# Sparse attention with large and small query tiles in turn, lower weight parts in pieces, last squares summed on TensorE

## The chip, the cores and the metric

The kernel runs on one core of a Trainium2 chip. The metric is device time in microseconds (us), the median of several executions of the whole program. Five queues work side by side: TensorE (PE, with its weight loads as PEld), VectorE (DVE), ScalarE (ACT), GpSimd (POOL) and SyncE (SP, which issues the DMAs).

## What is computed

One decoder layer on x of 1024 tokens by 1024 channels, in fp32: a norm, one input projection for three mixers (a chunked state-space scan, stick-breaking attention, sparse attention), gates that merge them, an output projection, a norm and a residual; then a gated MLP with a short convolution, and again a norm and a residual. Cut to the parts that the change touches:

```
def nsa_attention(...):            # sparse attention, 8 query heads, 2 key groups, head size 64
    ...
    imp = jnp.where(valid, jnp.where(forced, BIG, imp), NEG)
    _, idx = lax.top_k(imp, n_sel)             # 8 selected blocks of 64 keys
    p_sel = masked_softmax(ss, ...)            # over the selected blocks
    o_win = ... masked_softmax(sw, wmask) ...  # over a window of 512 keys
    out = gb[..., 0] * o_cmp + gb[..., 1] * o_sel + gb[..., 2] * o_win

def reference(...):
    ...
    x = x + rms_norm(mixed @ w_out[l], post_mix_norm[l])
    h = rms_norm(x, pre_ffn_norm[l])
    u = causal_dwconv(h @ ffn_w_up[l], ffn_conv_w[l], ffn_conv_b[l])
    gate, val = jnp.split(u, 2, axis=-1)
    f = (jax.nn.gelu(gate, approximate=True) * val) @ ffn_w_down[l]
    x = x + rms_norm(f, post_ffn_norm[l])
```

## The kernel before

Activations lie with channels on the partitions and tokens along the free axis, in halves of 512 tokens. A product of two fp32 matrices is made of three matmuls: each operand is split into an upper part (`hi`, rounded to TensorE's fp32 format) and a lower part (`lo`, the rest), and hi·hi, lo·hi and hi·lo are summed in PSUM. In the trace these are the matmuls called `dense`, 128x512 each.

**Weights.** `load_w` (line 278) brings a block of weights by a DMA of SP, makes `whi` on ACT (line 286) and `wlo` on POOL by one subtraction over the whole block (line 287): 78 blocks of 128x1024 and 16 of 128x512. A block of 1024 columns holds eight weight tiles of 128x128; its products take 24 matmuls, in which every third uses `wlo`. Some other weights have code of their own (`weights7`, from line 513); the change leaves that alone.

**Sparse attention** (`nsa_stage`, some 460 to 803 us). There are 16 query tiles of 128 queries: two key groups g, eight tiles i = 0 to 7 in each. Tile i attends to i + 1 blocks of 128 keys in the selected branch and to at most five in the window branch, so the tiles have 2, 4, 6, 8, 10, 11, 12 and 13 key blocks. Three pieces of program run interleaved, in an order written out by the loop over n behind line 1047: `attend` works on tile n (scores by TensorE, exponentials on ACT, `wT_lo` on POOL, products with the values on TensorE, merging on DVE), `maxima` on tile n + 1 and `compressed` on tile n + 2. `compressed` has the attention over compressed keys and, for i of 4 and more, the top-k chain on DVE (lines 888 to 900). `maxima` computes, for each head and branch, the products of queries and keys once more and takes their largest value on DVE (`mx`, line 955): 8 pieces for i below 4 and 16 for larger i; then `MM` (lines 962 and 963), three steps of delay (`MM_LAG`), four small transposes on TensorE and a copy into the rows of `Q` (line 969). Without these rows no score of the tile can start.

A tile gets max(9, its blocks) slots. In each slot `maxima` takes two steps and `compressed` one. What remains of either when the slots are over runs at once. Slots with no block are filled with matmuls of the merge gates' projection (`fill`, six matmuls, or three where a slot has a block and both other pieces are done); these wait for nothing in this stage. Instructions stand on each engine in the order in which the loop records them, so the order of the tiles sets what stands in front of what.

**Output projection, MLP and last norm** (`tail_stage`). `rstd` sums squares over the partitions with a matmul by ones, then takes Ln and Exp on ACT (lines 1483 and 1484) and three operations on DVE. The last part of the last product runs over three column groups, `LAST`, of 512, 256 and 256 columns. For each, eight output tiles j: the x add on DVE (line 1820), a square on ACT (1825), the sum of squares on DVE (1826), a scale on ACT (1827). `start_norm` of a group stands inside the next group's loop (the last one behind it): `norm_rows` turns the column sums into one number per token by small matmuls, takes the root on 128x2 or 128x4 values (lines 253 to 258), spreads it (1792) and transposes it back (`psn<-ident,u`); then eight multiplies on DVE (1803) and eight adds of the residual on POOL or DVE (1804), each followed by its DMA out.

Of the kernel before, what the change touches and what calls it, by code (L numbers as in the profile page):

```python
# [10 lines left out]
F32 = mybir.dt.float32  # L11
R32 = mybir.dt.float32r
BF = mybir.dt.bfloat16
AF = mybir.ActivationFunctionType
OP = mybir.AluOpType
# [4 lines left out]
T = 1024  # L20
DM = 1024
# [170 lines left out]
U0_BUFS = 6  # L192
U1_BUFS = 2
# [17 lines left out]
def trunk(ctx: ExitStack, tc: tile.TileContext, A: dict, outT: bass.AP, dbg=None):  # L211
    nc = tc.nc
    act = nc.scalar.activation
    V, P = nc.vector, nc.gpsimd
# [8 lines left out]
    mm, tr = pe(nc.tensor.matmul), pe(nc.tensor.transpose)  # L223

    def fl(ap):
        return ap.bitcast(F32)
# [54 lines left out]
    def load_w(src, n, tiles=None, raw=None):  # L281
        if raw is None:
            raw = wp.tile([128, n], F32, name="wraw", bufs=2)
        nc.sync.dma_start(raw, src)
        hi, lo = tiles or (wp.tile([128, n], R32, name="whi", bufs=2), wp.tile([128, n], R32, name="wlo", bufs=2))
        act(hi, raw, AF.Copy)  # L286
        (V if tiles else P).tensor_tensor(lo, raw, fl(hi), op=OP.subtract)  # L287
        return hi, lo

    def fm_unit(pool, w, rhs, nk, halves=(0, 1)):  # L290
# [76 lines left out]
    start = ExitStack()  # L367
# [97 lines left out]
    for h, tiles in ((0, [[ps_s, ps_s, ps_t, ps_t]]), (1, [[ps_o, ps_d], [ps_s, ps_s]])):  # L465
        *pss, ss = first_half(h, tiles)
        rq, r = norm(h, ss)
# [231 lines left out]
def nsa_stage(nc, tc, es, env):  # L699
    E = L(env)  # L700
    A, act, V, P, mm, tr, fl = E.A, E.act, E.V, E.P, E.mm, E.tr, E.fl
# [20 lines left out]
    start = ExitStack()  # L722
# [25 lines left out]
    for s in range(2):  # L748
# [33 lines left out]
        else:  # L782
            for g in range(2):
                mm(pk[:, g * 64:(g + 1) * 64], ht[:, g].rearrange("p a b -> p (a b)"), w2[:, 0, :],
                   start=True, stop=True)
# [258 lines left out]
                if b:  # L1044
                    value(*b)

    order = [(g, i) for g in range(2) for i in range(8)]
    res = {}
    E.in_order[0] = True
    att = attend()  # L1050
# [1 line left out]
    for n in range(-2, 17):  # L1052
# [3 lines left out]
        if 0 <= n < 16:  # L1056
            g, i = order[n]
# [28 lines left out]
    ps = ps_b()  # L1086
# [287 lines left out]
def tail_stage(nc, tc, es, env):  # L1374
    E = L(env)
    A, act, V, P, mm, tr, fl, pvc = E.A, E.act, E.V, E.P, E.mm, E.tr, E.fl, E.pvc
# [47 lines left out]
    for n, (br_i, k0, nk, src) in enumerate(((2, 12, 4, "wb_nsa"), (1, 8, 4, "wb_sb"), (0, 0, 8, "wb_ssm"))):  # L1424
# [3 lines left out]
        for j in range(8):  # L1428
# [3 lines left out]
            for h in range(2):  # L1432
# [7 lines left out]
                elif n == 2:  # L1440
                    P.tensor_tensor(b, part[h, j], b, op=OP.add)
                    hi, lo = mix[h, j] = hi_t(), lo_t()
                    act(hi, b, AF.Copy)
                    V.tensor_tensor(lo, b, fl(hi), op=OP.subtract)
        if n == 0:
# [4 lines left out]
            psn = es.enter_context(tc.tile_pool(name="psn", reuse_waits="tile", bufs=2, space=PSUM))  # L1450
# [3 lines left out]
    up_ = es.enter_context(tc.tile_pool(name="up", side="right", reuse_waits="tile", bufs=U_BUFS))  # L1454
# [6 lines left out]
    op = ExitStack()  # L1461
    ow = op.enter_context(tc.tile_pool(name="ow", reuse_waits="tile", bufs=2))
    rows = []
    for h in range(2):
# [25 lines left out]
        ss = [None]  # L1490
        for j in range(8):
            ps, = fm_unit(psd, load_w(A["wo"][j], 1024), lambda k, _: mix[h, k], 8, halves=(h,))
            act(o[j], ps, AF.Copy)
            sumsq(ss, ps)
        r = rstd(ss)
        ss, st = [None], [None]
# [8 lines left out]
        r = rstd(ss, st)  # L1505
        for j in range(9):
            if j < 8:
                i = V.scalar_tensor_tensor(o[j], o[j], pvc(PV_FFN, j), r, op0=OP.mult, op1=OP.mult)  # L1508
                tc.keep_in_program_order(i)
                hi, lo = h2[h, j] = hi_t(), lo_t()  # L1510
                act(hi, o[j], AF.Copy)
            if j > 0:
                hi, lo = h2[h, j - 1]
# [269 lines left out]
    def norm_rows(ss, W):  # L1783

        n = W // 128
        ps, r = [psn.tile([128, 512], F32, name="psn", tag="psn") for _ in range(2)]
        for m in range(n):
            mm(ps[:, m:m + 1], ss[:, m * 128:(m + 1) * 128], E.ones[:, 0:1], start=True, stop=True)
        rt, v = [fw.tile([128, 4], F32, name=f"r{x}", bufs=2) for x in "tv"]
        E.rsqrt_mean(rt[:, :n], v[:, :n], ps[:, :n], DM)  # L1790
        rb = up_.tile([128, 512], F32, name="u1", bufs=U1_BUFS)
        act(rb[:, :W].rearrange("p (n t) -> p n t", t=128), rt[:, :n, None].to_broadcast([128, n, 128]), AF.Copy)
        for m in range(n):
            tr(r[:, m * 128:(m + 1) * 128], rb[:, m * 128:(m + 1) * 128], E.ident)
        return r

    def start_norm(h, s, ss):
        W = s.stop - s.start
        r = norm_rows(ss, W)
        end = s.stop == 512 and h == 1  # L1800
        for j in range(8):
            a = acc[h][j][:, s]
            V.tensor_tensor(a, a, r[:, :W], op=OP.mult)  # L1803
            (P if j in T_POOL[end] else V).tensor_tensor(a, x1s[h][:, j, s], a, op=OP.add)
            nc.sync.dma_start(E.outT[j * 128:(j + 1) * 128, h * 512 + s.start:h * 512 + s.stop], a)

    for s0, s1 in LAST:
        h = s0 // 512
        s = slice(s0 - h * 512, s1 - h * 512)
        W = s1 - s0  # L1810
        ss = up_.tile([128, 512], F32, name="u0", bufs=U0_BUFS)
        for j in range(8):
            ps = bank()
            hi, lo = ws[j]
            for k in range(nf):
                for n, (a, b) in enumerate(((hi, 0), (hi, 1), (lo, 0))):
                    mm(ps[:, :W], a[:, k * 128:(k + 1) * 128], ms[k][h][b][:, s], start=k == 0 and n == 0,
                       stop=k == nf - 1 and n == 2)
            a = acc[h][j][:, s]
            V.tensor_tensor(a, a, ps[:, :W], op=OP.add)  # L1820
            if j == 0:
                act(ss[:, :W], a, AF.Square)
            else:
                sq = up_.tile([128, 512], F32, name="snap", bufs=SNAPS)
                act(sq[:, :W], a, AF.Square)
                V.tensor_tensor(ss[:, :W], ss[:, :W], sq[:, :W], op=OP.add)
            act(a, a, AF.Copy, scale=pvc(PV_PF, j))
            if j == T_AT and ended:
                start_norm(*ended)
                ended = None  # L1830
        ended = h, s, ss
    start_norm(*ended)


# [14 lines left out]
```

## Time and profile before

| | |
|---|---|
| median of 3 runs | 2268.85 us (2268.69 to 2269.64) |
| the profiled execution | 2272.78 us, of which the span of the trace is 2271.0 us |
| TensorE busy | 2176.9 us, 96% |
| VectorE, ScalarE, GpSimd busy | 1379.7 us (61%), 1202.8 us (53%), 1214.5 us (53%) |
| granted TensorE clock, mean | 0.985 of full |
| chain that ended last | PE 77%, DVE 12%, ACT 5%, issue 3%, POOL and DMA 1% each |

Times in the rows are from the start of the span. A busy TensorE is not the same as a TensorE at its peak: matmuls are pipelined, so the starts of successive ones tell the pace, not their durations. `out<-in` names what an instruction writes and reads. In brackets stands how long the engine was idle before the instruction and what ended that.

### The profile page before, as it was taken

How to read it: one execution, taken by the hardware profiler on the slowest of the kernel's cores; microseconds unless marked ns; L12 is line 12 of the kernel's file. 1: busy time of each engine (PE TensorE's matmuls, PEld its weight loads, DVE VectorE, ACT ScalarE, POOL GpSimd, SP SyncE). 2: the span in 40 equal slices, each digit the busy share in tenths (PEclk: the TensorE clock that was granted, in tenths of full speed). 3: DMA queues.
4: the chain of work that ended last, by engine and by line, in shares of the span. 5: the costliest groups of instructions: out<-in, count | busy, mean ns of one | idle time of the engine just before them, and what ended most of it. 6: DMA issues, size and time to landing. Idle time of an engine off the chain costs nothing.

```text
span 2271.0 us, 29865 instructions
## 1 busy us (share of the span) xinstructions
PE 2176.9 (96%) x10567; PEld 1735.8 (76%) x10567; DVE 1379.7 (61%) x2516; ACT 1202.8 (53%) x2240; POOL 1214.5 (53%) x867
## 2 busy tenths in 40 slices
PE   7999999998999999999999999999989999989997
PEld 7887889865666677878776678887668888868886
DVE  8665554258567526556636662349975766675786
ACT  7544443466756746666755531235544444465544
POOL 3776641246746733333337745446476777765743
PEclk9999999999999999999998999999999999999998
DMA  4233342321221011112362264235322323255433
GB/s 170 84 114 109 114 136 63 101 81 26 57 72 33 10 58 38 66 56 80 108 213 73 83 227 139 94 128 178 114 95 79 112 98 110 99 177 180 139 104 115
DMA packets 120103, 234.62 MB, mean 103 GB/s; under 512 B 28817, under 2 KB 43089, under 8 KB 119953
## 3 DMA queue, kind: packets, MB, share of 16 engines
q1 hardware_dynamic: 117072, 230.13, 30.8%
q10 hardware_dynamic: 2880, 2.59, 0.3%
q8 instruction: 83, 1.36, 0.3%
q14 instruction: 68, 0.55, 0.1%
HBM read 169.10 MB, written 63.57 MB: 102 GB/s over the span
## 4 chain that ended last, share of the span: by engine, by line
PE 77%; DVE 12%; ACT 5%; issue 3%; POOL 1%; DMA 1%; SPq 0%; DVEq 0%; ACTq 0%; POOLq 0%
PE dense L219 52%; PE ps_s L219 8%; PE ps_o L219 6%; PE ps_t L219 6%; PE ps_b L219 4%; PE psn L219 2%; DVE u L324 1%; DVE osq L1475 1%; DVE x L1502 1%; DVE mx L955 1%; DVE lo L1517 1%; DVE x L1662 1%; DVE x L1508 0%; DVE x L1803 0%; ACT h_hi L419 0%
## 5 line engine op out<-in xcount | busy, mean ns | idle before, releaser
L287 POOL TENSOR_TENSOR wlo<-wraw,whi 128x1024 fp32r<-128x1024 f32 (+1 forms) x94 | 213.4, 2270 | 296.0 <-ACT whi L286 295.1
L219 PE MATMUL dense<-h_hi,whi 128*128 128x512 f32 x656 | 263.2, 401 | 0.0
L219 PE MATMUL dense<-h_hi,wlo 128*128 128x512 f32 x656 | 257.4, 393 | 0.3 <-POOL wlo L529 0.3
L219 PE MATMUL dense<-h_lo,whi 128*128 128x512 f32 x656 | 257.3, 392 | 0.0
L993 POOL TENSOR_TENSOR wT_lo<-wT,wT_hi 128x512 fp32r<-128x512 f32 x132 | 168.1, 1285 | 98.5 <-ACT wT_hi L992 90.1
L219 PE MATMUL dense<-hi,whi 128*128 128x512 f32 x576 | 214.8, 393 | 0.5 <-ACT whi L286 0.5
L219 PE MATMUL dense<-hi,wlo 128*128 128x512 f32 x512 | 201.8, 397 | 7.8 <-POOL wlo L287 5.8
L219 PE MATMUL dense<-x,uhi 128*128 128x512 f32 x600 | 191.5, 392 | 1.2 <-ACT x L601 1.2
L219 PE MATMUL dense<-lo,whi 128*128 128x512 f32 x448 | 176.7, 394 | 1.9 <-DVE lo L1517 1.9
L286 ACT ACTIVATE whi<-wraw 128x1024 fp32r<-128x1024 f32 (+1 forms) x94 | 92.5, 984 | 159.2 <-PE dense L219 129.2
L538 POOL TENSOR_TENSOR ulo<-uf,uhi 128x1024 fp32r<-128x1024 f32 x38 | 92.2, 2426 | 113.2 <-ACT uhi L537 103.2
L219 PEld LDWEIGHTS dense<-h_hi,wlo 128*128 128x128 f32 x656 | 123.5, 188 | 27.3 <-POOL wlo L529 0.8
L219 PEld LDWEIGHTS dense<-h_hi,whi 128*128 128x128 f32 x656 | 124.1, 189 | 23.8
L219 PEld LDWEIGHTS dense<-h_lo,whi 128*128 128x128 f32 x656 | 123.8, 189 | 22.8
L1197 POOL TENSOR_TENSOR s_lo<-sa,s_hi 128x512 fp32r<-128x512 f32 (+2 forms) x48 | 53.4, 1114 | 153.6 <-ACT s_hi L1196 153.6
L219 PEld LDWEIGHTS dense<-x,uhi 128*128 128x128 f32 x600 | 113.0, 189 | 26.2 <-ACT x L601 2.5
L219 PEld LDWEIGHTS dense<-hi,whi 128*128 128x128 f32 x576 | 109.4, 190 | 24.9 <-ACT whi L286 1.2
L955 DVE TENSOR_REDUCE mx<-ps_t 128x1 f32<-128x384 f32 (+3 forms) x192 | 98.6, 520 | 47.0 <-PE ps_t L219 43.5
L324 DVE SCALAR_TENSOR_TENSOR u<-dense,pv,u 128x511 f32<-128x511 f32 (+1 forms) x140 | 103.5, 741 | 32.7 <-ACT u L320 32.7
L219 PEld LDWEIGHTS dense<-hi,wlo 128*128 128x128 f32 x512 | 97.2, 190 | 31.4 <-POOL wlo L287 8.1
L982 ACT ACTIVATE wT<-ps_s 128x512 f32<-128x512 f32 x132 | 78.3, 593 | 69.4 <-PE ps_s L219 64.4
L541 POOL TENSOR_TENSOR ulo<-uf,uhi 128x1024 fp32r<-128x1024 f32 x38 | 92.2, 2425 | 41.4 <-ACT uhi L540 39.4
(541 smaller groups left out, 6175.4 us busy)
## 6 DMA issues: line engine op xcount, KB each, us to landing
wraw<-in_wfm SPq DMA_DIRECT2D x62, 512.0 KB, 3.6
wraw<-in_wup SPq DMA_DIRECT2D x52, 512.0 KB, 3.6
lo<-m_d SPq DMA_DIRECT2D x58, 256.0 KB, 2.9
g_d<-gate_e SPq DMA_DIRECT2D x48, 256.0 KB, 2.2
s_d<-o SPq DMA_DIRECT2D x48, 256.0 KB, 2.0
ge<-g_d SPq DMA_DIRECT2D x24, 512.0 KB, 3.6
m_d<-u SPq DMA_DIRECT2D x44, 256.0 KB, 2.0
row<-s_d SPq DMA_DIRECT2D x16, 512.0 KB, 4.9
```

Source lines behind the costliest of these rows:

```text
L219: i = f(*a, **k)
L286: act(hi, raw, AF.Copy)
L287: (V if tiles else P).tensor_tensor(lo, raw, fl(hi), op=OP.subtract)
L324: V.scalar_tensor_tensor(o[:, d:], ps[:, :512 - d], taps[d], o[:, d:], op0=OP.mult, op1=OP.add)
L538: P.tensor_tensor(l24, f24, fl(h24), op=OP.subtract)
L541: P.tensor_tensor(l31, f31, fl(h31), op=OP.subtract)
L955: V.tensor_reduce(mx[:, h, a, n:n + 1], pm[:, :w], axis=AX, op=OP.max)
L982: act(w.rearrange("p h q -> p (h q)"), pz, AF.Exp)
L993: P.tensor_tensor(lo, wf, fl(hi), op=OP.subtract)
L1197: (P if SB_SLO else V).tensor_tensor(s_lo[:, c0:], a[:, c0:], fl(s_hi[:, c0:]), op=OP.subtract)
L1475: eng.tensor_tensor(sums[0], sums[0], sq, op=OP.add)
L1502: e.tensor_tensor(o[j], o[j], x, op=OP.add)
```

## The change

Three edits that don't depend on each other.

1. `load_w` subtracts in pieces of 256 columns where POOL does it: four instructions for a block of 1024, two for one of 512. On TensorE one `wlo` row of a block waited for POOL before; now every second `wlo` row does, each for its piece.
2. The order of the sparse attention's tiles within a group is 0, 4, 1, 5, 2, 6, 3, 7 in place of 0 to 7.
3. In the last column group (768 to 1024) TensorE sums the squares: eight matmuls by ones of 128x256 into one PSUM tile, the sum of tile j recorded behind the product of tile j + 1. The seven DVE adds go. `norm_wide` then works on 128x256 values in which every partition holds the same sums: three operations on ACT, three on DVE; the small matmuls, the spreading and the transposes of `norm_rows` go for this group.

```diff
@@ load_w
-        (V if tiles else P).tensor_tensor(lo, raw, fl(hi), op=OP.subtract)
+        w = n if tiles else 256
+        for c in range(0, n, w):
+            s = slice(c, c + w)
+            (V if tiles else P).tensor_tensor(lo[:, s], raw[:, s], fl(hi[:, s]), op=OP.subtract)
@@ nsa_stage
-    order = [(g, i) for g in range(2) for i in range(8)]
+    order = [(g, i) for g in range(2) for i in (0, 4, 1, 5, 2, 6, 3, 7)]
@@ tail_stage
+    def norm_wide(ps, W):
+        ps = ps[:, :W]
+        v = up_.tile([128, 512], F32, name="u1", bufs=U1_BUFS)[:, :W]
+        act(v, ps, AF.Identity, scale=1.0 / DM, bias=E.eps)
+        act(ps, ps, AF.Ln, scale=1.0 / DM, bias=E.eps)
+        act(ps, ps, AF.Exp, scale=-0.5)
+        V.tensor_tensor(v, v, ps, op=OP.mult)
+        V.scalar_tensor_tensor(v, v, -0.5, ps, op0=OP.mult, op1=OP.mult)
+        V.scalar_tensor_tensor(ps, v, 1.5, ps, op0=OP.add, op1=OP.mult)
+        return ps
...
-        ss = up_.tile([128, 512], F32, name="u0", bufs=U0_BUFS)
+        wide, sqs = s1 == T, []
+        if wide:
+            ss = psn.tile([128, 512], F32, name="psn", tag="psn")
+        else:
+            ss = up_.tile([128, 512], F32, name="u0", bufs=U0_BUFS)
+        def sum_up():
+            n = len(sqs) - 1
+            mm(ss[:, :W], E.ones, sqs[n][:, :W], start=n == 0, stop=n == 7, skip_group_check=True)
...
             V.tensor_tensor(a, a, ps[:, :W], op=OP.add)
+            if wide and j > 0:
+                sum_up()
...
+        if wide:
+            sum_up()
         ended = h, s, ss
-    start_norm(*ended)
+    start_norm(*ended, norm_wide)
```

**Where the instructions stand: TensorE at the start of a large tile.** `ps_s<-Q,K` are scores, `ps_t<-K,Q` with the masks are pieces of the maxima, `aug` and `MM` the transposes that fill rows of `Q`, `ps_o` the products with the values. Before, tile 3 (whose blocks are in the first two score rows) hands over to tile 4:

```order
L219 MATMUL ps_t<-K_1_3100,Q_4741 128x384
...
L219 MATMUL ps_t<-mask_d,ident_b 128x128
L219 MATMUL ps_s<-Q_4499,K_1_3100 128x512
L219 MATMUL ps_s<-Q_4500,K_1_3102 128x512
L219 LDWEIGHTS aug
L219 MATMUL ps_b<-ident_b,aug 32x128
...
L219 MATMUL ps_o<-wT_hi,V_hi 65x512
L219 MATMUL ps_o<-wT_hi,V_lo 65x512
L219 MATMUL ps_o<-wT_lo,V_hi 65x512
L219 LDWEIGHTS MM
L219 MATMUL ps_t<-ident_b,MM 32x128
...
L219 MATMUL ps_s<-Q_4741,K_0_3099 128x512
```

In the change, tile 0 hands over to tile 4:

```order
L219 MATMUL ps_t<-K_1_3109,Q_4126 128x384
...
L219 MATMUL ps_t<-mask_d,ident_b 128x128
L219 MATMUL ps_s<-Q_3940,K_1_3109 128x512
L219 MATMUL ps_s<-Q_3941,K_1_3111 128x512
L219 LDWEIGHTS aug
L219 MATMUL ps_b<-ident_b,aug 32x128
...
L219 LDWEIGHTS MM
L219 MATMUL ps_t<-ident_b,MM 32x128
...
L219 MATMUL ps_s<-Q_4126,K_0_3108 128x512
```

The three products `ps_o` between the transposes of `aug` and those of `MM` are not there; the first score follows `MM` directly in both. Tile 1 to 5 stands like tile 0 to 4; tiles 2 to 6 and 3 to 7 have the three `ps_o` rows as before. Each group thus has four places where a tile of nine slots is followed by one with 16 pieces of maxima; before, it had one (3 to 4).

**ScalarE where the output projection ends and the MLP begins.** `psn` are Ln (with `eps`) and Exp of the fourth `rstd`, `dense<-u` a gelu, `whi` the upper part of a block of weights. Before:

```order
L1545 ACTIVATE dense<-u_15108 128x512
L1483 ACT_TABLE_LOAD
L1483 ACTIVATE psn<-psn,eps 128x512
L1484 ACT_TABLE_LOAD
L1484 ACTIVATE psn<-psn 128x512
L1545 ACT_TABLE_LOAD
L1545 ACTIVATE dense<-u_15183 128x512
L286 ACTIVATE whi<-wraw 128x1024
```

In the change:

```order
L1550 ACT_TABLE_LOAD
L1550 ACTIVATE dense<-u_15238 128x512
L1550 ACTIVATE dense<-u_15319 128x512
L1488 ACT_TABLE_LOAD
L1488 ACTIVATE psn<-psn,eps 128x512
L1550 ACT_TABLE_LOAD
L1550 ACTIVATE dense<-u_15400 128x512
L286 ACTIVATE whi<-wraw 128x1024
L1489 ACT_TABLE_LOAD
L1489 ACTIVATE psn<-psn 128x512
```

A gelu, the upper part of a block and one more table load now stand between Ln and Exp, and that upper part has moved ahead of Exp.

**TensorE in the last column group.** `psn<-snap,ones` are the new sums, `psn<-ident,u` the transposes of the middle group's norm. In the change the end of TensorE's queue reads:

```order
L219 MATMUL dense<-lo,hi 128x256
L219 MATMUL psn<-snap,ones 128x256
L219 MATMUL dense<-hi,lo 128x256
...
L219 MATMUL dense<-lo,hi 128x256
L219 MATMUL psn<-snap,ones 128x256
L219 MATMUL dense<-hi,lo 128x256
...
L219 MATMUL dense<-lo,hi 128x256
L219 MATMUL dense<-hi,lo 128x256
L219 MATMUL psn<-ident,u_20897 128x128 x2
L219 MATMUL psn<-snap,ones 128x256 x2
```

Before, nothing stands between the `dense` rows of this group but the transposes and small sums of the groups ahead. Now six of the eight sums stand there, and two behind the last `dense` row.

## Rows read from the trace of the kernel before

**Rows 1.** The page, part 1: busy time and share of the span, TensorE.
```profile
PE 2176.9 (96%) x10567; PEld 1735.8 (76%) x10567; DVE 1379.7 (61%) x2516; ACT 1202.8 (53%) x2240; POOL 1214.5 (53%) x867
```

**Rows 2.** What TensorE waited for in 460 to 803 us: total, times, longest.
```profile
PE ps_t L219 <- DVE MM L963: 6.5, 8, 1.4
PE ps_t L219 <- DVE mx L955: 6.0, 11, 1.1
PE ps_s L219 <- DVE Q L969: 4.6, 4, 1.7
```

**Rows 3.** Windows by tile: length, then busy PE, PEld, DVE, ACT, POOL; tiles 1, 3.
```profile
475.00:492.00 17.00, 16.16 (x92) 11.40 (x91) 8.88 (x27) 11.24 (x26) 7.08 (x10) 1.00 0.18 52
...
511.00:529.00 18.00, 15.69 (x92) 10.26 (x91) 15.16 (x42) 12.85 (x30) 11.85 (x15) 1.00 0.11 30
```

**Rows 4.** Timeline, TensorE, tile 3 to 4: start, duration, line, operation, [idle before].
```profile
527.46 0.40 PE L219 MATMUL ps_t<-ident_b,MM 128*32 128x128 bf16 x4 [0.87 <-DVE MM L963]
528.64 0.73 PE L219 MATMUL ps_s<-Q,K 128*128 128x512 f32 x2 [0.79 <-DVE Q L969]
```

**Rows 5.** Timeline of VectorE at the same place.
```profile
525.78 0.69 DVE L930 CAST Q<-ps_b 32x512 fp32r<-32x512 bf16 x1 [0.30 <-PE ps_b L219]
...
527.22 0.18 DVE L963 SCALAR_TENSOR_TENSOR MM<-m,MM 128x8 bf16<-128x8 f32 x1
527.89 0.70 DVE L969 CAST Q<-ps_t 32x512 fp32r<-32x512 bf16 x1 [0.49 <-PE ps_t L219]
```

**Rows 6.** Windows at the lower clock (PEclk), one in each stage.
```profile
529.90:533.30 3.40, 3.40 (x13) 2.39 (x11) 2.07 (x8) 1.45 (x4) 1.27 (x1) 0.50 0.12 39
...
1612.00:1615.40 3.40, 3.40 (x9) 2.67 (x8) 3.40 (x6) 2.33 (x4) 3.40 (x4) 0.51 0.49 154
```

**Rows 7.** What TensorE waited for in 1355 to 1660 us.
```profile
PE dense L219 <- POOL wlo L287: 5.8, 5, 1.7
PE dense L219 <- DVE lo L1517: 1.9, 3, 1.4
PE psn L219 <- DVE osq L1475: 1.0, 1, 1.0
```

**Rows 8.** POOL's groups by shape, whole span: busy, mean ns, idle before.
```profile
L287 POOL TENSOR_TENSOR wlo<-wraw,whi 128x1024 fp32r<-128x1024 f32 x78 | 191.2, 2451 | 256.8 <-ACT whi L286 256.7
...
L1197 POOL TENSOR_TENSOR s_lo<-sa,s_hi 128x256 fp32r<-128x256 f32 x16 | 13.1, 822 | 39.7 <-ACT s_hi L1196 39.7
```

**Rows 9.** Line 287 on its engines: the same kind of subtraction on VectorE, late.
```profile
L287 DVE TENSOR_TENSOR lo<-snap,hi x4: 683/684/686, 2201.6 to 2205.7; 128x512 fp32r<-128x512 f32 x4
```

**Rows 10.** Timeline of VectorE after the longest wait for wlo.
```profile
1615.59 2.67 DVE L1517 TENSOR_TENSOR lo<-x,hi 128x512 fp32r<-128x512 f32 x1
```

**Rows 11.** Timeline of POOL there.
```profile
1615.31 2.40 POOL L287 TENSOR_TENSOR wlo<-wraw,whi 128x1024 fp32r<-128x1024 f32 x1
```

**Rows 12.** Timeline of ScalarE at the fourth rstd.
```profile
1603.95 1.28 ACT L1484 ACT_TABLE_LOAD   x1
...
1607.13 0.60 ACT L1545 ACTIVATE dense<-u 128x512 f32<-128x512 f32 x1
1607.67 1.04 ACT L286 ACTIVATE whi<-wraw 128x1024 fp32r<-128x1024 f32 x1
```

**Rows 13.** Timeline of TensorE around one sum by ones of 128x512.
```profile
1571.86 0.40 PE L219 MATMUL dense<-lo,whi 128*128 128x512 f32 x1
1572.10 1.02 PE L219 MATMUL psn<-osq,ones 128*128 128x512 f32 x2
...
1573.18 0.40 PE L219 MATMUL dense<-hi,whi 128*128 128x512 f32 x1
```

**Rows 14.** Timeline of TensorE, its last dense matmul.
```profile
2253.30 0.28 PE L219 MATMUL dense<-hi,lo 128*128 128x256 f32 x1
```

**Rows 15.** Timeline of VectorE at the end.
```profile
2256.38 0.43 DVE L1826 TENSOR_TENSOR u<-u,snap 128x256 f32<-128x256 f32 x1 [0.48 <-ACT snap L1825]
...
2262.60 2.74 DVE L1803 TENSOR_TENSOR x<-x,psn 128x256 f32<-128x256 f32 x8 [1.23 <-PE psn L219]
```

More of the change, by code (lines that the diff above doesn't have):

```diff
@@ L1795, in norm_rows, with start_norm @@
         return r
-    def start_norm(h, s, ss):
+    def norm_wide(ps, W):
[8 more added lines that the diff above has]
+        return ps
+    def start_norm(h, s, ss, norm):
         W = s.stop - s.start
-        r = norm_rows(ss, W)
+        r = norm(ss, W)
         end = s.stop == 512 and h == 1
@@ L1820, in tail_stage @@
             V.tensor_tensor(a, a, ps[:, :W], op=OP.add)
-            if j == 0:
-                act(ss[:, :W], a, AF.Square)
-            else:
+            if wide and j > 0:
+                sum_up()
+            if wide or j > 0:
                 sq = up_.tile([128, 512], F32, name="snap", bufs=SNAPS)
                 act(sq[:, :W], a, AF.Square)
-                V.tensor_tensor(ss[:, :W], ss[:, :W], sq[:, :W], op=OP.add)
+                if wide:
+                    sqs.append(sq)
+                else:
+                    V.tensor_tensor(ss[:, :W], ss[:, :W], sq[:, :W], op=OP.add)
+            else:
+                act(ss[:, :W], a, AF.Square)
             act(a, a, AF.Copy, scale=pvc(PV_PF, j))
             if j == T_AT and ended:
-                start_norm(*ended)
-                ended = None
+                start_norm(*ended, norm_rows)
+        if wide:
+            sum_up()
         ended = h, s, ss
-    start_norm(*ended)
+    start_norm(*ended, norm_wide)
 def kernel(**inputs):
```

## The prediction

> **What bounds the kernel now.** I read the page's busy times first: TensorE works 96% of the span [rows 1], so only what lengthens or shortens TensorE's own queue counts. A `dense` 128x512 starts every 0.23 to 0.24 us there [rows 13]; time is lost where a start comes late. So the views to read next are TensorE's waits, stage by stage. In the sparse attention all three large ones end with DVE: `MM` 6.5 us, `mx` 6.0, `Q` 4.6, together 17.1 of 343 us [rows 2]. They lie in tiles in which DVE is full: in tile 3's window DVE works 15.16 of 18 us and TensorE misses 2.3, in tile 1's it works 8.88 of 17 and TensorE misses 0.8 [rows 3]. Around the change of projections the waits are for `wlo` (5.8 us), for `lo` (1.9) and for the squares `osq` (1.0) [rows 7]. After some of these waits the granted clock is 0.50, the lower of the two levels (1.2 of 2.4 GHz), for 3.4 us [rows 6]; as all work then takes twice as long, one such stretch costs 1.7 us. There are three in the attention and two near the output projection. At the end the chain leaves TensorE: its last dense matmul starts at 2253.30 [rows 14], the last multiplies start at 2262.60 [rows 15].
>
> **The order of the tiles.** The instructions of a tile stay the same; what moves is which work shares a window.
>
> Price of a handover to a large tile: TensorE waits 0.87 us for `MM` and 0.79 for `Q` [rows 4], 1.66 together. DVE's rows show why: behind the transposes of `aug` comes a copy (0.69, from 525.78), then `m` and `MM` until 527.40, and the second copy (0.70) only when TensorE has transposed `MM` [rows 5]. That is a chain of latencies, not of load, and an emptier DVE shortens little of it. The change has eight such places in place of two like it. Four have the three `ps_o` products in between, as here; four don't, and lack some 0.7 us of cover (three starts at 0.23), so 1.66 + 0.7 = 2.35. An estimate of all: 4 x 1.66 + 4 x 2.35 = 16.0 us, against the 11.1 of `MM` and `Q` that it replaces (handovers to a small tile then cost about nothing, since its eight pieces are done long before): +4.9.
>
> What it gives back: DVE's top-k chain now falls into large tiles' windows that compute only eight pieces of maxima, so of the 6.0 us for `mx` I take 4 away. The clock's stretches I leave at three: more handovers, but up to 18 fill matmuls stand in the small tiles' windows, where tile 3 had none. Sum +0.9, call it **+1**. Bounds: below, `MM` and `Q` as now, `mx` gone and two of three stretches gone, -6.0 - 3.4 = -9.4; above, every handover with a stretch of its own (eight in place of three, 5 x 1.7 = 8.5) and `mx` doubled: 4.9 + 8.5 + 6.0 = +19.4. I take the value near the rows of the handovers that I can count. The keys' DMA that precedes tile 0's successor in group 1 keeps its place and isn't late.
>
> **Lower parts in pieces.** A subtraction of 128x1024 takes 2.45 us on POOL, one of 128x256 0.82 by the nearest row of that shape [rows 8], or 0.61 as a quarter of the whole. So the first piece is there 1.6 us earlier, and the block takes up to 3.3 in place of 2.45. TensorE needs a further piece only every six matmuls, 1.4 us, and POOL makes one in 0.82. The 5.8 us of five waits for `wlo`, the longest 1.7, are nearly gone: -5.6. POOL's extra work, 78 x 0.83 = 65 us for the large blocks, falls into the 257 us that it idles for `whi` before these very instructions [rows 8]; without that idle time it would delay `wT_lo` in the attention.
>
> The `lo` of the MLP's input is made on DVE. Alone such a subtraction takes 0.684 [rows 9]; at 1615.59 it took 2.67 [rows 10], while POOL ran a `wlo` of 2.40 from 1615.31 [rows 11]. The DVE operation ended when the other had, plus its own time: it stood still for the whole of it. With pieces it stands still for one piece, 0.8. So of 1.9 and 1.0 us I take two thirds, -1.9. The two stretches of low clock follow these waits: -3.4. Gross -10.9.
>
> Given back: the change puts a gelu, a `whi` and a table load between Ln and Exp of the fourth `rstd`: 0.60 + 1.04 + 1.28 = 2.92 us [rows 12], and the scaled activations, their `lo` and the first MLP product come that much later: +2.9 at most, as TensorE has other work for a part of it. DVE operations that slip in between two pieces delay the next: 1 us for all. Net **-7**, bounds -10.9 to 0. The Trainium skill has a rule that differs on the first of these: ScalarE: Activation LUTs, section Table sets, says that one set holds both Ln and Exp, so no load is needed between them, and that a load costs about 2.7 us. The trace has a load between them, of 1.28 [rows 12]; by the page's figure the net would be -5.6, and the measured one decides.
>
> **The last group.** Before, from the last dense start (2253.30) to the last multiplies (2262.60) lie 9.3 us: sums on DVE until 2256.8, the multiplies of the middle group, the small roots. In the change six sums by ones stand in front of TensorE's end. One of 128x512 takes 0.85 us (1.08 from 1572.10 to 1573.18, less one dense matmul of 0.23) [rows 13], so one of 128x256 some 0.43 and six 2.6: the dense work ends at 2256.2. Then one after the other: x add, square, sum, Identity, Ln, Exp and three DVE operations, nine steps at the 0.43 of a 128x256 row [rows 15] = 3.9, and some 0.4 between engines: 2260.5, where the multiplies start, in place of 2262.60. The middle group's multiplies (2.7 us) lie in that gap, while ACT works. So **-2**. Bounds: -4.7 if the sums hide in TensorE's waits, +1 if the last ones run at the lower clock and a table load slips in.
>
> **Sum.** +1 - 7 - 2 = -8 against the profiled execution's 2272.78: 2264.8. That execution stands 3.9 us above the median of the runs, so the median I expect is **2260.9, say 2261**. What a measurement of this kernel can tell from no change is about 0.2%, 4.5 us.
>
> **Rivals.**
> - *The order pays.* DVE's load evens out, `mx` no longer waits, two low-clock stretches go: -9.4 in place of +1, 2250.5. For it: all three waits are for DVE, and DVE's windows are far from even [rows 3]. Against: the chain at a handover is latency [rows 5]. Chance 0.17.
> - *The pieces give nothing.* Each piece is an instruction that a DVE operation with two SBUF inputs can get ahead of. Four times 0.82 + 0.68 = 6.0 us for a block in place of 2.45, 1.5 for a piece where TensorE wants one in 1.4; and Exp, 2.9 late, sets the start of the MLP. Then -1 in place of -7: 2267, within 0.2%. By the Trainium skill, SBUF - State Buffer, section Who interferes with whom, whichever of the two engines starts first holds the shared port for a whole instruction and the other blocks; the trace agrees with that for a long POOL instruction [rows 9 to 11], and what short ones in turn do no row here shows. Chance 0.2.
> - *Slower: the handovers.* Eight places where a tile starts with TensorE idle for 1.7 to 2.4 us, each followed by 3.4 us at the lower clock as at 529.9 [rows 6], and `mx` waiting twice as long because 16 pieces are squeezed into nine slots: +19.4 in place of +1, so 2279. It decides where DVE's share of a nine-slot window stays at or above the 0.84 of tile 3's. Against: no top-k falls into these windows any more, and they have fill. Chance 0.13.
> - *The change doesn't do what it says:* TensorE waits for a whole block all the same. Only the tail would be left, with the order at +1: about 2268. Against it stands the order of TensorE's instructions, in which every second `wlo` row waits for POOL. Chance 0.03.
>
> **How the numbers follow.** My forecast (2254 to 2266 with its own bounds) has 0.42, of which 0.40 lies below 2264.3 and so counts as faster; the order that pays 0.17, faster; the pieces that give nothing 0.2, of which 0.04 faster and 0.16 the same; the handovers 0.13, slower; 0.03 for the change that does nothing and 0.05 for the unforeseen, both the same. So faster 0.61, within 0.2% 0.26, slower 0.13. The range that leaves out the slow rival and the edges of the rest is 2247 to 2273.
>
> **What would show it.** Right: waits for `wlo` of line 291 under 1 us in all, DVE's `lo` under 1.6 us each, `MM` and `Q` waits of 14 to 18 us in eight pairs, `mx` about 2, the last multiplies at a distance of some 7 us behind the last dense matmul. Wrong: `MM` and `Q` at or below 11 us (then the order pays), low-clock stretches behind most handovers (then it costs), or new waits for `lo` or `x` of 2 us and more behind Exp (then the pieces give back what they gain).

## The result and the profile after

The changed kernel takes 2285.36 us (median of 4 runs, 2284.41 to 2287.76) against 2268.81 for the kernel before: a ratio of 1.0066, 95% interval 1.0053 to 1.0079. It is 16.5 us slower by the medians (15.0 by the ratio), where 8 us faster was forecast, and outside the range of 2247 to 2273. The profiled execution is 2285.28, so it stands at its median; that of before stood 3.9 above its own. The two traces therefore differ by 12.5 us.

Where the difference arises can be read by pairing the matmuls of the two traces, the n-th of a name and shape with the n-th, and comparing their starts: the changed kernel is 0.4 us behind at 450 us, 15.3 behind at 850, 11.8 at 1000, 18.6 at 1340, 15.2 at 1580, 16.4 from 1700 to 2000, 13.6 at 2240, and 12.5 at the end. Most is lost in the sparse attention, some in the state-space scan (1150 to 1340); a little comes back in the late stages.

Busy times on the page of the kernel after, to be read beside [rows 1]:

```profile
PE 2187.0 (96%) x10577; PEld 1742.7 (76%) x10577; DVE 1326.6 (58%) x2508; ACT 1207.7 (53%) x2241; POOL 1275.6 (56%) x1117
```

TensorE is busy 10 us longer; its share is the same. POOL's 61 us more are the pieces, close to the 65 worked out. What TensorE waits for in the attention, 455 to 815 us, to be read beside [rows 2] (total, times, longest):

```profile
PE ps_t L219 <- DVE MM L967: 13.0, 11, 1.9
PE ps_o L219 <- ACT oT L1010: 7.8, 9, 1.3
PE ps_s L219 <- DVE Q L973: 6.5, 8, 0.9
PE ps_s L219 <- DVE yacc L1023: 1.1, 3, 0.4
PE ps_b L219 <- ACT pT L911: 1.0, 2, 0.7
PE ps_s L219 <- ACT wT L986: 1.0, 3, 0.4
PE ps_t L219 <- DVE mx L959: 0.4, 2, 0.2
```

The waits for `mx` are nearly gone (6.0 to 0.4), as the even load of DVE should have it. `MM` and `Q` cost 19.5 us in place of 11.1, and a wait that was small, for `oT`, has grown to 7.8. TensorE's timeline at the first handover to a large tile, tile 0 to 4, beside [rows 4]:

```profile
472.19 0.40 PE L219 MATMUL ps_t<-ident_b,MM 128*32 128x128 bf16 x4 [1.50 <-DVE MM L967]
473.38 0.73 PE L219 MATMUL ps_s<-Q,K 128*128 128x512 f32 x2 [0.79 <-DVE Q L973]
```

And DVE's there, beside [rows 5]:

```profile
469.89 0.56 DVE L959 TENSOR_REDUCE mx<-ps_t 128x1 f32<-128x384 f32 x1 [1.66 <-PE ps_t L219]
470.73 0.69 DVE L934 CAST Q<-ps_b 32x512 fp32r<-32x512 bf16 x1 [0.29 <-PE ps_b L219]
...
471.96 0.18 DVE L967 SCALAR_TENSOR_TENSOR MM<-m,MM 128x8 bf16<-128x8 f32 x1
472.63 0.70 DVE L973 CAST Q<-ps_t 32x512 fp32r<-32x512 bf16 x1 [0.49 <-PE ps_t L219]
```

DVE was idle 1.66 us ahead of its last `mx`: it is not short of time at this place. Copy, `m`, `MM`, transposes and copy follow one another as before, and TensorE has nothing to do meanwhile: 1.50 + 0.79 us.

The windows of tiles 0, 4, 1 and 3, beside [rows 3] (length, then busy PE, PEld, DVE, ACT, POOL, then the clock):

```profile
460.80:473.40 12.60, 10.00 (x60) 7.28 (x59) 7.32 (x16) 7.18 (x12) 6.51 (x12) 1.00 0.32 99
473.40:500.40 27.00, 25.28 (x136) 18.22 (x136) 15.90 (x52) 16.91 (x43) 15.93 (x18) 0.94 0.14 37
500.40:517.10 16.70, 14.12 (x82) 9.93 (x82) 10.90 (x28) 9.00 (x19) 6.35 (x10) 1.00 0.14 39
588.50:606.10 17.60, 15.79 (x93) 10.39 (x92) 14.28 (x33) 12.86 (x30) 11.26 (x14) 1.00 0.18 47
```

DVE's share in these four is 0.58 to 0.81, below the 0.84 of tile 3 before, and TensorE still misses 2.6, 1.7, 2.6 and 1.8 us. An even DVE doesn't keep TensorE busy. The end of the kernel, first TensorE's last dense matmul (beside [rows 14]), then DVE's timeline (beside [rows 15]):

```profile
2269.43 0.29 PE L219 MATMUL dense<-hi,lo 128*128 128x256 f32 x1
```

```profile
2269.75 0.42 DVE L1847 TENSOR_TENSOR x<-x,dense 128x256 f32<-128x256 f32 x1 [1.45 <-PE dense L219]
2270.09 2.73 DVE L1820 TENSOR_TENSOR x<-x,psn 128x256 f32<-128x256 f32 x8
...
2273.64 0.43 DVE L1811 SCALAR_TENSOR_TENSOR psn<-u,psn 128x256 f32<-128x256 f32 x1
2274.10 2.73 DVE L1820 TENSOR_TENSOR x<-x,psn 128x256 f32<-128x256 f32 x8
```

### The profile page after: what moved, and what is told of

It reads as the page before. It is cut to its first block, busy times and chain, and to the rows that moved or that the text cites. A ratio compares the mean times of both kernels' runs of the same rounds, so it can differ in the third digit from the quotient of the medians.

```text
span 2283.6 us, 30185 instructions
## 1 busy us (share of the span) xinstructions
PE 2187.0 (96%) x10577; PEld 1742.7 (76%) x10577; DVE 1326.6 (58%) x2508; ACT 1207.7 (53%) x2241; POOL 1275.6 (56%) x1117
## 3 DMA queue, kind: packets, MB, share of 16 engines
q8 instruction: 83, 1.36, 0.3%
## 4 chain that ended last, share of the span: by engine, by line
PE 79%; DVE 7%; ACT 5%; issue 4%; POOL 3%; DMA 2%; SPq 0%; DVEq 0%; ACTq 0%; POOLq 0%
PE dense L219 54%; PE ps_s L219 7%; PE ps_o L219 6%; PE ps_t L219 6%; PE ps_b L219 3%; PE psn L219 2%; POOL wlo L291 0%; ACT wT L986 0%; ACT h_hi L423 0%; DMA traw<-in_wtm 0%; DVE x L1667 0%; POOL alo L547 0%; DVE u L328 0%; DMA s_d<-o 0%; POOL wlo L533 0%
## 5 line engine op out<-in xcount | busy, mean ns | idle before, releaser
L291 POOL TENSOR_TENSOR wlo<-wraw,whi 128x256 fp32r<-128x256 f32 x344 | 276.7, 835 | 265.3 <-ACT whi L286 264.1
L328 DVE SCALAR_TENSOR_TENSOR u<-dense,pv,u 128x510 f32<-128x510 f32 (+1 forms) x140 | 103.3, 741 | 36.5 <-ACT u L324 36.4
```

What stands on the lines that cost most here:

```text
L291: (V if tiles else P).tensor_tensor(lo[:, s], raw[:, s], fl(hi[:, s]), op=OP.subtract)
L328: V.scalar_tensor_tensor(o[:, d:], ps[:, :512 - d], taps[d], o[:, d:], op0=OP.mult, op1=OP.add)
```

## The experiments

Each variant is compared with runs of the kernel before on the same chip at the same time; the median of those is 2269 to 2272 us. Single executions of one kernel scatter by 4 to 6 us to either side. The 95% intervals of the ratios are 2 to 3 us wide to either side where a variant has 10 or 12 runs, and 3 to 7 where it has 4 to 6. Many variants ran on different chips, so the distance between two of them is less sure than that of each from before.

### The three edits apart

Theory: the order of the tiles costs, in the attention itself, because each handover to a large tile is a chain without cover. Rival: the pieces on POOL cost it.

`order_only`:

```diff
-    order = [(g, i) for g in range(2) for i in range(8)]
+    order = [(g, i) for g in range(2) for i in (0, 4, 1, 5, 2, 6, 3, 7)]
```

> The kernel before with the new order of the tiles alone. Theory (the order costs, in the attention itself): 12 to 17 us slower than before, waits for MM and Q together 18 to 20 us, for oT 7 to 8, for mx under 1, three or more low-clock stretches behind handovers; no shift between 1150 and 1300 us beyond what the attention leaves. Rival (the pieces on POOL cost most of the loss, the order little): at most 8 us slower.

Measured: 2283.77 against 2269.46, ratio 1.0063 (1.0048 to 1.0078). `pieces_only` has just the loop over 256 columns in `load_w`.

> The kernel before with the lower parts in pieces alone. Theory (the order costs): between 6 us faster and 2 us slower, with about 5 us gained from 1340 us on and a loss of up to 6 between 1150 and 1300, where POOL has the state-space scan's work. Rival (the pieces cost): 6 to 12 us slower, and the attention's waits grow with it.

Measured: 2268.32, ratio 0.9998 (0.9986 to 1.0010). `last_only` has `norm_wide` and the sums on TensorE.

> The kernel before with the last group's squares summed on TensorE alone. Both theories: 1 to 3 us faster, all of it behind 2250 us; a second theory, that the sums cost TensorE what DVE gains, gives no change within 1 us.

Measured: 2267.76, ratio 0.9989 (0.9979 to 0.9998). `pieces_last` is the changed kernel with the old order.

> The changed kernel with the old order of the tiles. Theory (the order costs, and the parts add up): 0 to 8 us faster than before, that is 16 to 24 us faster than the change. Rival (the pieces cost): 4 to 10 us slower than before.

Measured: 2268.65, ratio 0.9994 (0.9984 to 1.0004). The order alone makes nearly the whole loss, 14.3 of 16.5 us. Together the three parts make 12.6 us; the rest lies within their intervals. The rival falls. The last group gives about 1.7 us, the pieces nothing that these runs can tell.

### What the order costs

The waits of `order_only`, from the stage's start until 850 us:

```profile
PE ps_t L219 <- DVE MM L963: 13.5, 11, 2.5
PE ps_o L219 <- ACT oT L1006: 7.8, 9, 1.3
PE ps_s L219 <- DVE Q L969: 6.5, 8, 0.9
PE dense L219 <- DVE row L1121: 2.2, 1, 2.2
PE ps_s L219 <- DVE yacc L1019: 1.5, 4, 0.4
...
PE ps_t L219 <- DVE mx L955: 0.4, 2, 0.2
```

And the wait for `oT` before, 460 to 803 us:

```profile
PE ps_o L219 <- ACT oT L1006: 2.8, 7, 1.4
```

Against [rows 2]: `MM` +7.0 and `Q` +1.9; `oT` +5.0; `mx` -5.6; the smaller ones together about even. That is some +8 inside the stage. Behind it a wait of 2.2 for `row` is new. The lower clock covers three stretches of 3.4 us before (at 529.9, 707.4 and 731.3) and 17.1 us in `order_only` (6.8 from 473.4, 3.4 from 637.2, 6.8 from 661.1), two of them right behind the first handover of a group. The first of these in a window of `order_only`, with the clock of 0.50 third from the end:

```profile
473.40:480.20 6.80, 6.28 (x25) 5.20 (x25) 3.76 (x13) 2.73 (x5) 3.57 (x4) 0.50 0.14 47
```

7 us more at half speed are 3.4 lost. Together some 14, of 14.3 measured. The clock's term is the least sure: in the ten traces of kernels whose attention stands as before, the stage has 3.4 to 13.7 us at the lower clock, so one trace against one can be 2 us off here by chance.

If missing cover is the cause, cover must help. `order_slots12` gives each tile 12 slots at least:

```diff
-NSA_SLOTS = 9
+NSA_SLOTS = 12
```

> The new order alone, with at least 12 slots for a tile in place of 9, so that 16 pieces of maxima and the three steps behind them fit, and three slots more per small tile are filled with gate matmuls taken from later. Theory (a squeezed handover is what the order costs): waits for MM and Q together fall from 20 us to under 9, and the time is 8 to 12 us below that of the order alone, 2272 to 2276. Rival (DVE can't keep up with 16 pieces in a small tile): the waits turn into waits for mx, and at most 3 us are gained.

Measured: 2289.75, ratio 1.0098 (1.0075 to 1.0121): 6 us above `order_only`, though `MM` fell from 13.5 to 7.9 and `Q` from 6.5 to nearly nothing. Neither theory had this. The windows of group 0, of group 1 and of the 25 us behind the stage, `dense` matmuls alone (length, busy PE with their number, the clock):

```profile
471.70:681.90 210.20, 73.50 (x273) 1.00 0.20 59
681.90:833.50 151.60, 8.35 (x33) 0.99 0.10 28
833.50:858.50 25.00, 12.00 (x46) 0.80 0.03 10
```

The gate matmuls ran out: 273 in group 0 and 33 in group 1, where `order_only` has 135 in each. The first group did lose waits (12.9 us in all, 17.4 in `order_only`), the second paid for it (17.3 against 13.8), and so did the stretch behind the stage: TensorE has only 46 dense matmuls there, against 91 in the same 25 us of `order_only`, and runs at 0.80 of the clock. The fill is a fixed stock, and work taken forward is missing later. Two more variants move the fill or the load:

`order_fill21`: `NSA_FILL = (2, 1)`, three matmuls in every slot that has a block.

> The new order alone, with three gate matmuls also in every slot that has a key block. Theory (a large tile has lost its cover, since its window now computes only eight pieces of maxima): waits for oT fall from 7.8 us to under 3, those for yacc and wT vanish, MM and Q shrink little; 3 to 6 us below the order alone, 2278 to 2281. Rival (the wait for oT is ACT's load, not missing cover): the matmuls only move the wait, within 2 us of the order alone.

Measured: 2288.61, ratio 1.0088 (1.0056 to 1.0119); `oT` 3.5, `Q` 6.5, and again no gate matmul in group 1. `order_ot_dve`: the copy of `oT` by `V.tensor_copy` in place of `act(..., AF.Copy)`.

> The new order alone, with the copy oT made on DVE in place of ACT. Theory (oT stands in ACT's queue behind the eight softmax steps cp of a tile of compressed keys, for which the one PSUM bank of ps_o waits): waits for oT fall from 7.8 us to under 3, time 3 to 6 us below the order alone. Rival (the copy is late because its product is late): they stay at 6 us or more, time the same.

Measured: 2287.36, ratio 1.0090 (1.0059 to 1.0121). No wait for `oT` is left among the large ones, so it did stand in ACT's queue, but `MM` grew from 13.5 to 16.6 and waits for DVE's `left` (1.9) and `yacc` appeared. The expected gain of 3 to 6 us didn't come: the wait was moved to DVE.

`order_slots10`: as `order_slots12` with 10.

> The new order alone, with at least 10 slots for a tile: 48 gate matmuls more in the stage, fewer than the 78 that were left behind it, so that they don't run out as with 12 slots. Theory (handovers without cover): MM and Q from 20 us to under 13, no tile without gate matmuls that had them, 3 to 7 us below the order alone. Rival (gate matmuls used here are missing behind the stage): the stage gains, the stretch from 818 us on loses as much, time within 2 us of the order alone.

Measured: 2280.23, ratio 1.0050 (1.0035 to 1.0064), 3.5 us below the order alone by the medians; the intervals of the two overlap. `MM` and `Q` 13.6 (of which `Q` rose to 9.4, the wait having moved one step on), and the gate matmuls ran out again at the end. The time is inside the theory's numbers, the waits are a little above its 13, and its claim that the stock would do is wrong.

The clean test keeps the number of gate matmuls and moves only their place. `order_early` packs the blocks of a nine-slot tile so that its last slot is empty:

```diff
+        if 0 < nb < slots:
+            it = iter([q for q in blocks if q])
+            cnt = slots - 1
+            blocks = [next(it) if m * nb % cnt < nb else None for m in range(cnt)] + [None]
```

> The new order alone, with the key blocks of tiles of nine slots placed so that the last slot is empty: its six gate matmuls now stand between the last maxima and MM. The number of gate matmuls is the same. Theory (a handover is a chain of latencies without cover): waits for MM fall from 13.5 us to under 6, those for Q stay at 6 to 7, oT falls as well since a small tile's last product comes earlier; 6 to 10 us below the order alone, 2274 to 2278. Rival (the time goes where the work is, any cover is taken from another place): within 2 us of the order alone, other waits in the place of MM.

Measured: 2277.72, ratio 1.0047 (1.0029 to 1.0065): below the order alone by 6 us by the medians and by 3.6 by the ratios, whose intervals overlap. Its waits, 455 to 830 us:

```profile
PE ps_s L219 <- DVE Q L969: 7.7, 9, 0.9
PE ps_t L219 <- DVE MM L963: 7.2, 9, 2.5
PE ps_b L219 <- DVE yacc L913: 3.2, 2, 1.6
PE ps_s L219 <- ACT wT L982: 3.2, 5, 1.6
PE ps_o L219 <- ACT oT L1006: 1.7, 5, 0.6
```

`MM` fell from 13.5 to 7.2 and `oT` from 7.8 to 1.7, `Q` rose a little (6.5 to 7.7), as its copy has no cover in this version either. Cover at the handover does take those waits away, as the theory has it, though `MM` at 7.2 is above the 6 expected. The rival has its part too: `yacc`, `wT` and others grew, and all waits of TensorE from 455 to 850 us fell only from 33.8 to 29.6. A part of the gain may be the clock's: 10.2 us at the lower level up to 850 us in this trace, 17.1 in that of `order_only`. The same placing in the old order:

> The kernel before, old order, with the same placing of the key blocks. Theory: its waits for MM fall from 6.5 us to under 3; 2 to 5 us faster than before. Rival: within 1.5 us of before.

Measured: 2279.89, ratio 1.0052 (1.0039 to 1.0065), 10 us slower than before, against the expectation. `MM` fell (6.5 to 4.3) but `mx` rose to 8.7, `Q` to 6.1 and `oT` to 5.5. The likely reading is that cover moved to the end of a tile is taken from its middle, and that in the old order few handovers had needed it; which of the new waits comes from which block was not tried. With the last group's sums:

> The kernel before, old order, with the key blocks placed early and the last group's squares summed on TensorE. Theory: the gains add up, 3 to 7 us faster than before. Rival: the last group alone, 1 to 2 us faster.

Measured: 2282.18, ratio 1.0056 (1.0041 to 1.0071). It misses as well.

### What the pieces cost

In `pieces_only` the five waits for `wlo` of [rows 7] are gone but for one of 0.4, and there is a new one of 3.03 us at 1634.34. TensorE's timeline there, and POOL's:

```profile
1634.34 0.54 PE L219 MATMUL dense<-hi,wlo 128*128 128x512 f32 x1 [3.03 <-POOL wlo L290]
```

```profile
1630.60 3.69 POOL L290 TENSOR_TENSOR wlo<-wraw,whi 128x256 fp32r<-128x256 f32 x1 [6.04 <-ACT whi L286]
```

DVE's:

```profile
1630.00 1.89 DVE L562 TENSOR_TENSOR x<-x 128x512 f32<-128x512 f32 x3
1631.81 0.68 DVE L564 TENSOR_TENSOR x<-x 128x512 f32<-128x512 f32 x1
1632.41 1.28 DVE L563 TENSOR_TENSOR x<-x 128x512 f32<-128x512 f32 x2
1633.61 0.74 DVE L327 SCALAR_TENSOR_TENSOR u<-dense,pv,u 128x511 f32<-128x511 f32 x1
```

A piece that takes 0.74 us alone took 3.69. DVE runs operations with two SBUF inputs back to back until 1633.6; the next one reads PSUM, and 0.7 us later the piece is done. So it is not that each piece loses one turn, as the rival had it: one piece lost all of them, and the next longest of the 344 took 1.8. The same piece took 3.97 us in the changed kernel (at 1645.0) and 3.84 in `pieces_late` (1624.9), each time behind the same run of DVE's operations.

`pieces_late` has pieces only for the output projection's and the MLP's weights, so that all ahead stands as before:

```diff
-            ps, = fm_unit(psd, load_w(A["wo"][j], 1024), ...)
+            ps, = fm_unit(psd, load_w(A["wo"][j], 1024, piece=256), ...)
```

and the same for `wup`.

> The kernel before with pieces only for the weights of the output projection and of the MLP's first product; everything ahead of 1560 us stands in the order of before. Theory (pieces gain about 3 us where TensorE waits for wlo and lose about 5 between 1150 and 1300, where the scheduler has placed the instructions differently for the longer POOL work): no loss between 1150 and 1300, 2 to 4 us faster than before. Rival (what the pieces gain at wlo they give back at the wait of 3 us for a later wlo and at uhi): within 1.5 us of before.

Measured: 2267.71, ratio 0.9997 (0.9986 to 1.0008): as the rival had it, with its wait of 3.2 for `wlo`. `late128` has `piece=128` in both places.

> As pieces_late, with pieces of 128 columns, eight for a block. Theory (where DVE runs operations with two SBUF inputs back to back, a piece stands still behind them, and each further piece is a new chance to lose): at the place where pieces of 256 took 6.7 us for a block, the block takes 8 us or more, the longest wait for wlo grows from 3.2 us to 4 or more; time 0 to 4 us above pieces_late. Rival (the wait there comes from whi on ACT, whatever the pieces): the wait stays at 3.0 to 3.4, time within 1 us of pieces_late.

Measured: 2265.32, ratio 0.9984 (0.9974 to 0.9993). The longest wait for `wlo` is 1.4 in place of 3.2 and the time is not above that of `pieces_late`, so the theory's price for more pieces falls. What it says of POOL happened all the same at another place: a piece of 128 columns that takes 0.46 us alone took 3.97 at 1579.11, beside six DVE operations `x<-x,ox` in a row, and TensorE waited for nothing there. `late512`:

> As pieces_late, with pieces of 512 columns, two for a block. Theory: the longest wait for wlo falls below 2 us, and since the first piece is there after 1.3 us the other waits for wlo stay small, under 2 us together; 1 to 3 us faster than pieces_late. Rival: the wait stays at 3.0 to 3.4, time within 1 us of pieces_late.

Measured: 2267.21, ratio 0.9986 (0.9976 to 0.9995). Waits for `wlo` 3.0 in all, the longest 1.4. The waits that come are of different kinds in each: `late128` waits 3.8 for POOL's `lo`, `late512` 4.5 for DVE's `x` and 2.0 for its `lo`. By the ratios the three sizes gain 0.7, 3.6 and 3.2 us (256, 128 and 512 columns), and their intervals overlap.

`pieces_ahead` is the complement, pieces everywhere but in those two places.

> The kernel before with pieces of 256 columns everywhere but in the output projection and the MLP's first product, the complement of pieces_late. Theory (pieces cost in the stages ahead, where the scheduler then places the scan's instructions differently): 1 to 5 us slower than before, and the scan takes 3 to 7 us longer than before's 183 from its first to the first product of the branch projections. Rival (the longer scan in three earlier profiles was the clock's chance): within 1 us of before, the scan at 180 to 185 us.

Measured: 2271.78 against 2271.54, ratio 1.0000 (0.9990 to 1.0010): as the rival has it in time. But the scan is longer in this trace, as the theory has it. Its first matmul and the first product behind it, before:

```profile
1156.21 0.49 PE L219 MATMUL ps_s<-half,sel 16*128 16x512 f32 x1
```

```profile
1338.90 0.63 PE L219 MATMUL dense<-hi,whi 128*128 128x512 f32 x2
```

and in `pieces_ahead`:

```profile
1149.88 0.49 PE L219 MATMUL ps_s<-half,sel 16*128 16x512 f32 x1
```

```profile
1338.60 0.63 PE L219 MATMUL dense<-hi,whi 128*128 128x512 f32 x2
```

182.7 us before and 188.7 there. More than half of this can be the clock: 17.1 us of the scan are at the lower level before and 23.9 there, which is 3.4 us lost of the 6.0. In the four kernels with pieces ahead of the scan it takes 184.9 to 189.5 us. Of the fifteen without, fourteen take 177.8 to 184.1, and `order_fill21` takes 188.4.

The scheduler has placed the scan's instructions in another order, and it is not the pieces alone that do this. TensorE's order in the scan is the same in `pieces_only`, `pieces_last` and `pieces_ahead` and also in `order_fill21` and `order_ot_dve`, which have no pieces: 182.9 to 188.9 us in these five. In the ten kernels with the order of before it takes 177.8 to 183.4. So the longer scan goes with the order in which it stands, and pieces are one of several edits that bring that order about.

By the rows paired with before, the kernels with pieces ahead gain some 3.5 us between 890 and 980 and lose them and more in the scan. Of the 3.5 a part is a stretch at the lower clock that before has at 977.1 and these don't; the rest are two shorter waits of the stick-breaking attention (1.36 and 2.24 before, 0.43 and 1.29 in `pieces_ahead`).

### The version that is fastest

`last_late512`: the old order, the last group's sums on TensorE, pieces of 512 columns late.

> The kernel before, old order, with pieces of 512 columns late and the last group's squares summed on TensorE. Theory: the gains add up, 2 to 5 us faster than before. Rival (what the pieces gain is given back): 1 to 2 us faster, as the last group alone.

Measured: 2264.59 against 2270.16, ratio 0.9979 (0.9967 to 0.9990): about 5 us faster than before, and 20 faster than the change. With 128 columns:

> The kernel before, old order, with pieces of 128 columns late and the last group's squares summed on TensorE. Theory (pieces of any size gain 2 to 4 us in the late stage if nothing ahead of it is moved, and the last group 1 to 2): 3 to 7 us faster than before. Rival (what the pieces gain is given back): 1 to 2 us faster, as the last group alone.

Measured: 2267.23 against 2271.54, ratio 0.9983 (0.9973 to 0.9993). The two don't differ by more than the runs scatter.

## Why the prediction was wrong

**The order of the tiles, +1 forecast, +14.3 measured.** This term failed, in four places.

*The handovers.* The estimate was 16.0 us for `MM` and `Q`, and 20.0 were measured in `order_only`. The price of one was right (0.8 to 0.9 for `Q` in all eight; in the changed kernel 1.5 for `MM` without `ps_o`, 0.6 to 1.0 with it, where I had 1.56 and 0.87), and there are eight, which together cost 15.5. What I set to nothing, the handovers to small tiles, has the other 4.5: three waits for `MM`, the longest 2.5. The waits for `mx` fell by 5.6 where I took 4 away; that was right in kind.

*The new wait for `oT`, 5.0.* It is not in the sum at all. I had looked at what the maxima of the next large tile cost in a small tile's window, and not at what they had covered in a large one's. With only eight pieces in its window, TensorE reaches the large tile's first product, which needs the one bank of `ps_o`, while the copy `oT` of the small tile's last product still stands in ACT's queue behind the softmax steps `cp`. TensorE's wait in the changed kernel, and ACT's timeline ahead of it (two of the eight `cp` rows):

```profile
481.59 0.45 PE L219 MATMUL ps_o<-wT_hi,V_hi 128*65 128x512 f32 x1 [1.26 <-ACT oT L1010]
```

```profile
479.12 0.34 ACT L882 ACTIVATE cp<-cp,m 128x64 f32<-128x64 f32 x1
...
480.35 0.19 ACT L882 ACTIVATION_READ_ACCUMULATOR cp<-cp,m 128x1 f32 x1
480.45 0.61 ACT L996 ACTIVATE wT_hi<-wT 128x512 fp32r<-128x512 f32 x1
480.96 0.57 ACT L1010 ACTIVATE oT<-ps_o 65x512 f32<-65x512 f32 x1
```

*The clock.* I left three stretches, because up to 18 fill matmuls stand in the small tiles' windows; 17.1 us at the lower level came. The 18 are there, but not where the gap is. In the changed kernel the last one in tile 0's window starts 3.7 us ahead of the handover at 472.19, and the clock falls at 474.6:

```profile
468.51 0.40 PE L219 MATMUL dense<-h_hi,wlo 128*128 128x512 f32 x1
```

*The 2.2 us behind the stage.* They were not in the sum either. `order_only` has used 270 gate matmuls between its first and its last score where before has used 252, which is the likely reason; no run tried it alone.

The rival on the slower side had the mechanism, eight handovers and the clock behind some of them, and gave 2279 with a price for `mx` that didn't come. By its own condition, DVE's share at or above 0.84, it should not have come true, as the four windows above show. I gave it 0.13 and put weight on DVE's share, which fell as forecast and decided nothing.

**The pieces, -7 forecast, 0 measured.** Three steps of this sum failed, all seen in `pieces_only`. The first is the 5.6 us for `wlo`: the five waits did go, but for 0.4, and the new one of 3.0 came, so 2.4 were gained. That wait was among the rivals, with 1.5 us for a piece; one piece took 3.7. The second is the 3.4 us for two stretches at the lower clock, which I took to follow the waits. They came again, at 1617.6 and 1634.7:

```profile
1617.60:1621.00 3.40, 3.14 (x8) 1.98 (x7) 3.40 (x7) 3.05 (x6) 3.40 (x4) 0.50 0.25 99
```

The third is that the sum had nothing for the scan, which takes 6.2 us more in that trace; 3.4 of them can be the lower clock's, as in `pieces_ahead`. I had read the moved instructions around the output projection and passed over those in the scan, which the order lists as well. The other terms were right: `osq` waits less (1.0 to 0.2), the waits for DVE's `lo` are gone, and what was to be given back was. From Ln to Exp of the fourth `rstd` it takes 4.89 us in place of 1.97, the 2.92 more that I had added up from [rows 12], and behind it TensorE waits 1.1 us for `hi` and 0.9 for `lo`. In all, 3.3 us are gained between 1340 and 1700 us, about 3.5 between 890 and 980, and 6.2 lost in the scan between them.

**The last group, -2 forecast, -1.7 measured** (by the medians; -2.5 by the ratio, -0.5 to -4.8 by its interval). As worked out, six of the sums stand in front of TensorE's end, and the multiplies follow the last dense matmul at 4.7 us (2269.43 and 2274.10) in place of 9.3. I gave "some 7 us" as a sign, which did not follow from my own steps (4.3); the sign was wrong, the term right. The Trainium skill's rule on one table set for Ln and Exp (ScalarE: Activation LUTs, section Table sets) is what the new chain shows: Identity, Ln and Exp follow each other and no load stands between them, unlike at [rows 12]. ACT's timeline:

```profile
2271.41 0.47 ACT L1806 ACTIVATE u<-psn,eps 128x256 f32<-128x256 f32 x1 [0.25 <-PE psn L219]
2271.78 0.44 ACT L1807 ACTIVATE psn<-psn,eps 128x256 f32<-128x256 f32 x1
2272.25 0.37 ACT L1808 ACTIVATE psn<-psn 128x256 f32<-128x256 f32 x1
```

**What stays open.** Why the lower clock comes behind the handover from tile 0 to 4 of each group and not behind most others. Which instruction of the scan makes it longer, and how much of that is the clock; no run tried it. And a good part of the pieces' late gain, 0.7 to 3.6 us by size, lies within what the runs scatter.

## What to carry to other kernels

Matmuls that wait for nothing are a stock: count how many there are, and put them where a chain of latencies stands between two pieces of work. Evening out the busiest helper engine buys only the waits for its load, not those for its latency; before moving work out of a window, ask what it covered there. A change that adds or moves instructions can reorder a stage that it doesn't touch, so read the difference of the order in all stages, and time each edit apart.

## What was not expected of the hardware

One POOL subtraction of 128x256 took 3.69 us in place of 0.74 while DVE ran operations with two SBUF inputs back to back, and one of 128x128 took 3.97 in place of 0.46 in `late128`. The Trainium skill (SBUF - State Buffer, section Who interferes with whom) says that whoever starts first holds the shared port for its whole instruction; that alone would give one turn's wait of some 0.6 us here, and the runs show a piece that waits through five or six turns of the other engine.
